# A two-mixer block with PEER experts: three edits of order and place, one of rate, one of sign

## The chip, the cores and the metric

The kernel runs on one core of a Trainium2 chip. The metric is the device time of one execution in microseconds (us). The engines are TensorE (PE, with its weight loads as PEld), VectorE (DVE), ScalarE (ACT) and GpSimd (POOL); SyncE (SP) and POOL issue the transfers. Each engine takes its own instructions strictly in the order in which they were laid down when the program was built.

## What the kernel computes

One layer over 512 tokens of width 1024, in float32. Sub-layer 1 is a norm, one wide projection, chunked band attention with a relative-position bias (8 heads of 64), an mLSTM (4 heads of 128), two gates and an output projection. Sub-layer 2 is a PEER layer: product keys choose 16 of 16,384 single-neuron experts per token and head.

```
s  = einsum("blhd,bkhd->bhlk", qj, kj) * scale + bias     # band attention
p  = softmax(where(valid, s, -inf))
...
q  = (xb @ w_pq).reshape(128, 8, 2, 128)                  # PEER, by blocks of 128 tokens
s_top, i_top = top_k(einsum("thpd,hpnd->thpn", q, sub_keys), 16)
best, ci     = top_k(s_top[:,:,0,:,None] + s_top[:,:,1,None,:], 16)
e    = i1 * 128 + i2                                      # i1, i2: the keys behind ci
gate = softmax(best)
act  = gelu(einsum("thkd,td->thk", u_exp[e], xb))
out  = rmsnorm(x + gt2 * einsum("thk,thkd->td", gate * act, v_exp[e]), final_g)
```

## The kernel before

Every float32 product on TensorE is made of three products of split operands: a tile is cast to a high part (`split`, line 147, ACT) and the rest is subtracted from it (line 150, DVE or POOL, tile `wlo`), and `mm3` (lines 160 to 162) multiplies high by high, high by low and low by high.

The first sub-layer takes the first 450 us or so. `mixer_a` does the attention, two heads per projection. For each head it loads a 128x512 bias, masks a corner of it with a memset (line 333), and for each of four row tiles adds bias and scores with a running maximum (line 343), negates the maximum (line 347), and exponentiates with it as the bias of the activation (line 349). The bias tile has two buffers.

The second sub-layer runs the experts in two ways. For tokens 160 to 511, 128 dense blocks, one per value of the first key, compute all 128 experts of the block (`hidden`: load `u_t[e]`, split, 24 matmuls into a 128x352 tile `ps_act`, gelu) and weigh them with a table of gates. For the other tokens rows of `u` and `v` are fetched one expert per token at a time, by an indirect transfer on POOL's queue (`row`, line 704) and a DVE instruction over 128x1024 elements for each (lines 712 and 761); the row buffers `ur` are five. The stages:

- `scores` finds the top experts, head by head. In `select` two masks of 128x1024 elements are multiplied on POOL (lines 691 and 699), with DVE instructions before and after each.
- `build` makes the gate table of 128 tokens: 32 steps for each of three token tiles (order 2, 3, 1). In each step DVE compares four tokens' first keys with an iota (line 781, tile `o4`), DVE, POOL and ACT make the second factor (lines 792 to 796, tile `oa`), TensorE multiplies (line 798, `ps_g`), ACT copies (line 799). Eight steps fill one buffer `gst`, which POOL's queue writes to memory `gd` (line 804).
- `ahead` does `hidden` for blocks 0 to 63 beside these two stages and stores the gelus in memory (`ad`). `paced` takes blocks at RATE_S = 1.1 per step of `scores` (17 steps, so 18 blocks), three more after it, and RATE_B = 0.4 per step of `build` (12 for each tile). 57 blocks are taken by then, and the last seven follow in a loop of their own (line 986), each with one step of the row gather `gathered(cp, 0)`.
- `output` goes over all 128 blocks, eight new ones (64 and up: "hot", `hidden` runs now, into one of two `ew` buffers of two blocks each) and eight stored ones ("cold") in turn. For each eight it loads a slice `gq` of the gate table from `gd` (line 844, SP's queue, two buffers), multiplies gelus and gates (line 859), splits them (lines 863 and 864), loads and splits `v_e[e]` (tile `vst`), and adds 18 matmuls of 128x512 to six accumulators. After each block it yields HOT = 2.6 or COLD = 1.25, the number of row steps that `paced` takes then.
- `finish` adds the residual to a token tile, norms and stores it. Tile 0 comes from the rows (259 steps: one for the index, 128 for `u`, one for the gelu, 128 for `v`, one for `finish`), tiles 1 to 3 from the accumulators, after the last block. Each call takes two 128x1024 buffers, `o` and `xr`, from the five of `ur`; two more hold `gt2` and the final gain from the first call on.

A list scheduler with a cost model lays down each engine's instructions: by order in the code where several are ready, otherwise whichever is ready, so that instructions may pass one another. `tc.issue_after(x)` keeps each instruction that it encloses, on the engine of x, behind x. `slowly(g)` runs a generator's steps under it with `state["mark"]`, which is the newest `wlo` of DVE.

Of the kernel before, what the change touches and what calls it, by code (L numbers as in the profile page):

```python
# [37 lines left out]
GG = 8  # L38
VST, UR = 3, 5
TG = 32  # L40
NR = P // TG
# [7 lines left out]
OAP, OAD, TWO = 8, 12, 4  # L49
RATE_S, TOP, RATE_G, RATE_B, RATE_0, RATE_A, HOT, COLD = 1.1, 3, 0.62, 0.4, 0.8, 1.0, 2.6, 1.25  # L50
WST, WB, VB = 4, 3, 3
# [23 lines left out]
def drive(*gens):  # L75
    for _ in weave(*gens):
        pass
# [3 lines left out]
def tile_block(  # L81
# [232 lines left out]
    def mixer_a(ap, hT, va, y_hi, y_lo):  # L314
# [7 lines left out]
        for hp in range(4):  # L322
            ps = bank("acc", "ps_qa")
            proj_t(ps, piece("qa", hp), hT)
            qaT = ap.tile([P, S], F32, tag="qaT", name="qaT", bufs=2)
            nc.scalar.mul(qaT, ps, 0.125)
            psy = bank("acc", "ps_ya")
            for hh in range(2):
                h = 2 * hp + hh
                po = 64 * hh  # L330
                bias = ap.tile([P, S], F32, tag="bias", name="bias", bufs=2)
                nc.sync.dma_start(bias, rel[h])
                nc.vector.memset(bias[:64, S - 64 :], NEG)
                for qt in range(4):
                    n = (qt + 1) * P
                    cs = slice(qt * P, n)
                    pss = bank("w", "ps_s")
                    nc.tensor.matmul(
                        pss[:, :n], qaT[po : po + 64, cs], kaT[po : po + 64, hp, :n], start=True, stop=True
                    )  # L340
                    sb = ap.tile([P, S], F32, tag="sb", name="sb", bufs=3)
                    mx = ap.tile([P, 1], F32, tag="mx", name="mx", bufs=3)
                    nc.vector.tensor_tensor_reduce(
                        out=sb[:, :n], in0=pss[:, :n], in1=bias[:, S - n :], scale=1.0, scalar=LOWEST,
                        op0=ALU.add, op1=ALU.max, accum_out=mx,
                    )
                    nc.vector.tensor_scalar_mul(mx, mx, -1.0)
                    sm = ap.tile([P, 1], F32, tag="sm", name="sm", bufs=3)
                    nc.scalar.activation(sb[:, :n], sb[:, :n], AF.Exp, bias=mx, accum_out=sm)
                    nc.vector.reciprocal(sm, sm)  # L350
                    nc.vector.tensor_scalar_mul(sb[:, :n], sb[:, :n], sm)
                    pst = bank("g", "ps_pt")
                    for kt in range(qt + 1):
                        nc.tensor.transpose(pst[:, kt * P : (kt + 1) * P], sb[:, kt * P : (kt + 1) * P], ident)
                    pt = ap.tile([P, S], F32, tag="pt", name="pt", bufs=2)
                    nc.scalar.copy(pt[:, :n], pst[:, :n])
                    for kt in range(qt + 1):
                        nc.tensor.matmul(
                            psy[po : po + 64, cs],
                            va[:, kt, h * 64 : (h + 1) * 64],  # L360
                            pt[:, kt * P : (kt + 1) * P],
                            start=kt == 0,
                            stop=kt == qt,
                        )
                    if qt % 2:
                        yield
            nc.scalar.copy(y_hi[:, 0, hp, :], psy)
            nc.vector.tensor_sub(y_lo[:, 0, hp, :], psy, y_hi[:, 0, hp, :].bitcast(F32))
            yield
# [283 lines left out]
    def select(cp, h, sv, i16, best, slots):  # L653
# [36 lines left out]
        nc.vector.tensor_tensor(out=m, in0=bc(pf), in1=bq(C_OFF), op=ALU.is_ge)  # L690
        nc.gpsimd.tensor_mul(q, m, bs(dl))
        both = cp.tile([P, 4, TOPK], F32, tag="both", name="both")
# [5 lines left out]
        nc.vector.tensor_tensor(out=m, in0=bc(of), in1=bq(C_SEQ), op=ALU.is_equal)  # L698
        nc.gpsimd.tensor_mul(m, m, bs(idx[:, :, 1, :]))
        nc.vector.tensor_reduce(slots[:, :, 1, h], m, axis=AX.X, op=ALU.add)  # L700
# [65 lines left out]
    def build(cp, i, slots):  # L766
# [8 lines left out]
        for b in range(P // TB):  # L775
            st = cp.tile([P, P, TB], F32, tag="gst", name="gst", bufs=2)
            for t4 in range(TB // 4):
                ps = bank("gw"[t4 % 2], "ps_g")
                o4 = cp.tile([P, 4, P], F32, tag="two", name="o4", bufs=TWO)
                t0 = b * TB + t4 * 4  # L780
                nc.vector.tensor_tensor(
                    out=o4, in0=iota.unsqueeze(1).broadcast_to([P, 4, P]),
# [31 lines left out]
    def ahead(up, h2T):  # L814

        for e in range(E1):
# [3 lines left out]
            if e % EG == EG - 1:  # L820
                nc.sync.dma_start(ad[e // EG], g)
            yield

    def output(cp, vp, h2T):
# [50 lines left out]
        for i in range(nt):  # L875
            with tc.issue_after(last.ins) if i else nullcontext():
                for n in range(2):
                    for x in late:
                        last = rows_of_v(i, n, *x)
            finish(cp, 1 + i, acc[2 * i : 2 * i + 2])  # L880

    def finish(cp, i, halves):

# [4 lines left out]
        gt2, fgb = state["rows"]  # L888
        o = cp.tile([P, D], F32, tag="ur", name="o", bufs=UR)
        xr = cp.tile([P, D], F32, tag="ur", name="xr", bufs=UR)  # L890
        nc.sync.dma_start(xr, x2d[i])
# [53 lines left out]
    def slowly(g):  # L945

        while True:
# [4 lines left out]
            yield  # L952

    def paced(main, *sides):

# [9 lines left out]
    with pool("epool") as cp:  # L965
# [3 lines left out]
        with pool("dpool") as dp, pool("upool") as up:  # L969
# [9 lines left out]
            for i in (2, 3, 1):  # L979
# [5 lines left out]
                drive((paced(build(dp, i, state["slots"][:, i]), (side, RATE_B), own), 1))  # L985
            drive((paced(side, (slowly(gather), RATE_A)), 1))
        if stop == "u":
# [76 lines left out]
```

## Time and profile before

| | |
|---|---|
| median of 3 runs | 1746.39 us |
| lowest, highest | 1742.57, 1746.93 us |
| profiled execution: its time | 1740.86 us |
| profiled execution: span, first to last instruction | 1739.1 us |
| PE busy in it | 1664.5 us (96%) |
| DVE, ACT, POOL busy | 1342.4, 769.4, 632.5 us |
| bytes moved | 441.00 MB |

Busy time of PE says that matmuls were under way, not that they ran at their best rate. The granted clock is the share of full speed (2.4 GHz) that TensorE was given; half of it is its other level, 1.2 GHz. The DMA share is the mean busy share of the core's 16 DMA engines. A number behind an arrow in square brackets is the time for which the engine stood idle just before, and what ended it.

### The profile page before, as it was taken

Reading aid. Unit: us, or ns where it says so; the run is one execution under the profiler, and the core shown is the slowest. Engines: PE = TensorE matmul, PEld = TensorE weight load, DVE = VectorE, ACT = ScalarE, POOL = GpSimd, SP = SyncE. Lnnn points to the kernel's source line nnn. Section 1 sums busy time; section 2 is a strip of 40 time slices with the busy share of each in tenths; the row PEclk is TensorE's granted clock in tenths of the full one; section 3 lists DMA queues with packets and bytes.
Section 4 is the critical chain, followed back from the end, with each engine's and each line's share of the span. In section 5 each row is a group of like instructions: output and inputs, shape, how many; then the busy total and the mean of one; then the engine's idle time right before and its main releaser. Section 6 shows DMA issues by size and latency. Waiting matters only on the chain.

```text
span 1739.1 us, 24668 instructions
## 1 busy us (share of the span) xinstructions
PE 1664.5 (96%) x8679; PEld 1446.8 (83%) x8679; DVE 1342.4 (77%) x2750; ACT 769.4 (44%) x1406; POOL 632.5 (36%) x524
## 2 busy tenths in 40 slices
PE   5999999999899998899999899999999999999996
PEld 4766678878789887899999788888888988888885
DVE  7467565675559999899798678787877878787896
ACT  4544545433453333889586233333333333333333
POOL 0000000000147765957483234444434434444450
PEclk9999999999999999999999899999999999999998
DMA  8524234572332333789979989999989999899984
GB/s 299 163 73 139 67 98 133 173 250 98 113 116 93 119 119 131 276 335 353 391 293 369 398 305 339 351 336 338 343 328 345 354 325 356 313 370 328 328 306 181
DMA packets 139166, 441.00 MB, mean 254 GB/s; under 512 B 15041, under 2 KB 41793, under 8 KB 137506
## 3 DMA queue, kind: packets, MB, share of 16 engines
q1 hardware_dynamic: 95842, 263.25, 43.4%
q0 software_dynamic: 43200, 176.18, 27.0%
q8 instruction: 68, 1.11, 0.3%
q14 instruction: 56, 0.46, 0.1%
HBM read 398.05 MB, written 40.90 MB: 252 GB/s over the span
## 4 chain that ended last, share of the span: by engine, by line
PE 55%; DVE 10%; DMA 3%; POOL 3%; issue 2%; ACT 0%; SPq 0%; DVEq 0%; POOLq 0%; ACTq 0%
PE acc L160 10%; PE acc L162 10%; PE acc L161 10%; PE ps_act L160 7%; PE ps_act L162 7%; PE ps_act L161 7%; PE ps_g L798 3%; DMA vst<-in_v_e 1%; DVE wlo L150 1%; POOL oa L796 1%; DMA ur<-in_u_r,eg 1%; DVE i L648 1%; DVE sc L649 1%; DVE i L651 1%; DMA gd<-gst 1%
## 5 line engine op out<-in xcount | busy, mean ns | idle before, releaser
L147 ACT CAST whi<-wst 128x512 fp32r<-128x512 f32 (+1 forms) x301 | 222.6, 771 | 402.2 <-PE ps_act L161 192.3
L162 PE MATMUL ps_act<-h2T_hi,wlo 128*128 128x352 f32 x1024 | 338.7, 331 | 14.6 <-DVE wlo L150 8.4
L160 PE MATMUL ps_act<-h2T_hi,whi 128*128 128x352 f32 x1024 | 337.0, 329 | 7.9 <-ACT ew L812 7.9
L161 PE MATMUL ps_act<-h2T_lo,whi 128*128 128x352 f32 x1024 | 337.0, 329 | 0.0
L150 DVE TENSOR_TENSOR wlo<-wst,whi 128x512 fp32r<-128x512 f32 (+1 forms) x251 | 235.0, 951 | 98.4 <-ACT whi L147 95.6
L161 PE MATMUL acc<-wlo,ehi 128*128 128x512 f32 x768 | 299.5, 390 | 0.0
L162 PE MATMUL acc<-whi,elo 128*128 128x512 f32 x768 | 290.4, 390 | 0.0
L704 POOL DMA_INDIRECT ur<-in_u_r,ei x128 | 181.0, 1414 | 252.5 <-DVE junk L712 222.1
L704 POOL DMA_INDIRECT ur<-in_v_r,ei x128 | 185.1, 1446 | 209.3 <-DVE sum_v L761 191.2
L160 PE MATMUL acc<-whi,ehi 128*128 128x512 f32 x768 | 252.7, 391 | 0.0
L162 PEld LDWEIGHTS ps_act<-h2T_hi,wlo 128*128 128x128 f32 x1024 | 195.5, 191 | 21.2 <-DVE wlo L150 10.7
L712 DVE SCALAR_TENSOR_TENSOR junk<-ur,h 128x1024 bf16<-128x1024 f32 x160 | 195.4, 1221 | 19.9 <-DMA ur<-in_u_r,eg 11.5
L160 PEld LDWEIGHTS ps_act<-h2T_hi,whi 128*128 128x128 f32 x1024 | 195.7, 191 | 12.2 <-ACT ew L812 8.5
L161 PEld LDWEIGHTS ps_act<-h2T_lo,whi 128*128 128x128 f32 x1024 | 195.6, 191 | 3.8
L150 DVE TENSOR_TENSOR wlo<-vst,whi 128x1024 fp32r<-128x1024 f32 x128 | 155.7, 1222 | 25.8 <-ACT whi L147 25.6
L147 ACT CAST whi<-vst 128x1024 fp32r<-128x1024 f32 x128 | 132.2, 1047 | 94.7 <-PE acc L162 39.9
L161 PEld LDWEIGHTS acc<-wlo,ehi 128*128 128x128 f32 x768 | 144.2, 188 | 28.6
L162 PEld LDWEIGHTS acc<-whi,elo 128*128 128x128 f32 x768 | 144.0, 188 | 28.7
L160 PEld LDWEIGHTS acc<-whi,ehi 128*128 128x128 f32 x768 | 142.9, 188 | 26.6
L761 DVE SCALAR_TENSOR_TENSOR sum_v<-ur,act,sum_v 128x1024 f32<-128x1024 f32 x127 | 163.0, 1283 | 1.7 <-DMA ur<-in_v_r,ei 0.6
L863 ACT CAST ehi<-gq 128x768 fp32r<-128x768 f32 x64 | 53.4, 837 | 233.4 <-PE acc L161 199.9
L150 POOL TENSOR_TENSOR wlo<-wst,whi 128x512 fp32r<-128x512 f32 x50 | 67.3, 1361 | 163.3 <-ACT whi L147 163.3
(302 smaller groups left out, 2856.7 us busy)
## 6 DMA issues: line engine op xcount, KB each, us to landing
wst<-in_u_t SPq DMA_DIRECT2D x128, 512.0 KB, 5.5
vst<-in_v_e SPq DMA_DIRECT2D x128, 512.0 KB, 6.7
wst<-in_w_pieces SPq DMA_DIRECT2D x76, 512.0 KB, 3.7
wst<-in_w_ada SPq DMA_DIRECT2D x48, 512.0 KB, 3.4
gd<-gst POOLq DMA_DIRECT2D x12, 2048.0 KB, 10.6
gq<-gd SPq DMA_DIRECT2D x16, 1536.0 KB, 12.3
ad<-gelu SPq DMA_DIRECT2D x16, 704.0 KB, 6.6
aq<-ad SPq DMA_DIRECT2D x16, 704.0 KB, 7.3
```

The costliest lines, as they stand in the source:

```text
L147: nc.scalar.copy(hi[:, cs], t[:, cs])
L150: ins = e.tensor_tensor(out=lo[:, cs], in0=t[:, cs], in1=hi[:, cs].bitcast(F32), op=ALU.subtract)
L160: nc.tensor.matmul(o, a[0], b[0], start=first, stop=False)
L161: nc.tensor.matmul(o, a[0], b[1], start=False, stop=False)
L162: return nc.tensor.matmul(o, a[1], b[0], start=False, stop=last)
L648: nc.vector.max_index(places[:, :8], vals[:, :8], data)
L649: nc.vector.match_replace(data, vals[:, :8], data, LOWEST)
L704: nc.gpsimd.indirect_dma_start(out=t, out_offset=None, in_=src, in_offset=bass.IndirectOffsetOnAxis(ap=ei[:, j : j + 1], axis=0))
L712: nc.vector.scalar_tensor_tensor(junk(), row(cp, u_r, ei, j), 1.0, h2, op0=ALU.mult, op1=ALU.mult, accum_out=act[:, j : j + 1])
L761: nc.vector.scalar_tensor_tensor(sum_v, t, act[:, j : j + 1], sum_v, op0=ALU.mult, op1=ALU.add)
L798: nc.tensor.matmul(ps[:, tt::4], oa, ob, start=True, stop=True)
L863: nc.scalar.copy(whb, w)
```

## The change

It has five parts.

1. The last three blocks of `ahead` (`BACK`) are taken in a loop of their own without row steps. In it every DVE instruction stands behind the last compare of the last table (line 781, now kept as `state["built"]`). Four blocks, not seven, are left for the loop with row steps.
2. HOT goes from 2.6 to 2.85 and COLD from 1.25 to 1.4.
3. In `finish` for token tiles 2 and 3 the two buffers `o` and `xr` are the halves of a buffer `gq` instead of two of the `ur`.
4. In `select` the two multiplications of the last head go to DVE.
5. The attention works with negated scores: the query is scaled by -0.125, the bias is negated by POOL after its load, the maximum becomes a minimum, the exponential gets scale -1, and the negation of the maximum is dropped. The corner's memset goes to POOL.

```diff
+TG, BACK = 32, 3
-... HOT, COLD = ... 2.6, 1.25
+... HOT, COLD = ... 2.85, 1.4
 # mixer_a
-            nc.scalar.mul(qaT, ps, 0.125)
+            nc.scalar.mul(qaT, ps, -0.125)
...
-                nc.vector.memset(bias[:64, S - 64 :], NEG)
+                nc.gpsimd.tensor_scalar_mul(bias, bias, -1.0)
+                nc.gpsimd.memset(bias[:64, S - 64 :], -NEG)
...
-                        out=sb[:, :n], in0=pss[:, :n], in1=bias[:, S - n :], scale=1.0, scalar=LOWEST,
-                        op0=ALU.add, op1=ALU.max, accum_out=mx,
+                        out=sb[:, :n], in0=pss[:, :n], in1=bias[:, S - n :], scale=1.0, scalar=-LOWEST,
+                        op0=ALU.add, op1=ALU.min, accum_out=mx,
                     )
-                    nc.vector.tensor_scalar_mul(mx, mx, -1.0)
-                    nc.scalar.activation(sb[:, :n], sb[:, :n], AF.Exp, bias=mx, accum_out=sm)
+                    nc.scalar.activation(sb[:, :n], sb[:, :n], AF.Exp, scale=-1.0, bias=mx, accum_out=sm)
 # select
-        nc.gpsimd.tensor_mul(q, m, bs(dl))
+        e = nc.vector if h == 7 else nc.gpsimd
+        e.tensor_mul(q, m, bs(dl))
...
-        nc.gpsimd.tensor_mul(m, m, bs(idx[:, :, 1, :]))
+        e.tensor_mul(m, m, bs(idx[:, :, 1, :]))
 # build
-                nc.vector.tensor_tensor(
+                state["built"] = nc.vector.tensor_tensor(
 # ahead
+            state["ahead"] = e + 1
             yield
 # output
-            finish(cp, 1 + i, acc[2 * i : 2 * i + 2])
+            room = None
+            if i:
+                gq = vp.tile([P, nb, GG, TB], F32, tag="gq", name="gq")
+                room = [gq[:, 4 * j : 4 * j + 4].rearrange("p b i t -> p (b i t)") for j in range(2)]
+            finish(cp, 1 + i, acc[2 * i : 2 * i + 2], room)
 # finish(cp, i, halves, room=None)
-        o = cp.tile([P, D], F32, tag="ur", name="o", bufs=UR)
-        xr = cp.tile([P, D], F32, tag="ur", name="xr", bufs=UR)
+        o, xr = room or [cp.tile([P, D], F32, tag="ur", name=nm, bufs=UR) for nm in ("o", "xr")]
+    def until(g, e):
+        while state["ahead"] < e:
+            yield next(g)
 # the main sequence
-            drive((paced(side, (slowly(gather), RATE_A)), 1))
+            drive((paced(until(side, E1 - BACK), (slowly(gather), RATE_A)), 1))
+            state["mark"] = state["built"].ins
+            drive((slowly(side), 1))
```

## Rows read from the trace of the kernel before

**Rows 1.** The page's first line: span and instructions.

```profile
span 1739.1 us, 24668 instructions
```

**Rows 2.** Stretches: us, busy of PE, PEld, DVE, ACT, POOL; clock; DMA share; GB/s.

```profile
100.00:250.00 150.00, 144.56 (x661) 99.37 (x661) 95.27 (x298) 70.39 (x182) 1.27 (x2) 0.97 0.29 92
...
941.00:985.00 44.00, 34.43 (x188) 33.09 (x188) 27.56 (x35) 14.61 (x20) 15.03 (x12) 0.88 1.03 385
985.00:1719.00 734.00, 734.00 (x3634) 642.89 (x3633) 588.65 (x631) 255.17 (x306) 314.76 (x219) 1.00 0.92 333
1650.00:1700.00 50.00, 50.00 (x251) 43.88 (x250) 46.46 (x41) 16.25 (x20) 27.60 (x20) 1.00 0.86 303
1719.00:1739.10 20.10, 6.52 (x29) 5.07 (x27) 12.41 (x24) 5.23 (x15) 0.00 (x0) 0.76 0.36 127
...
970.00:980.00 10.00, 4.24 (x14) 4.24 (x15) 5.92 (x7) 5.49 (x8) 0.63 (x1) 0.58 1.06 379
...
800.00:850.00 50.00, 50.00 (x361) 49.78 (x362) 49.06 (x97) 41.82 (x97) 25.88 (x23) 1.00 1.01 401
```

**Rows 3.** Instructions in order of time on PE, 945 to 985: those after idle time.

```profile
951.18 0.43 PE L160 MATMUL ps_act<-h2T_hi,whi 128*128 128x352 f32 x1 [1.34 <-ACT ew L812]
...
965.43 0.43 PE L162 MATMUL ps_act<-h2T_hi,wlo 128*128 128x352 f32 x1 [1.66 <-DVE wlo L150]
...
975.76 0.66 PE L160 MATMUL ps_act<-h2T_hi,whi 128*128 128x352 f32 x1 [6.57 <-ACT ew L812]
```

**Rows 4.** Instructions in order of time on DVE, 915 to 1000.

```profile
926.15 1.22 DVE L150 TENSOR_TENSOR wlo<-wst,whi 128x1024 fp32r<-128x1024 f32 x1
...
932.93 0.68 DVE L781 TENSOR_TENSOR o<-iota,sT 128x512 f32<-128x512 f32 x1
...
933.79 1.21 DVE L150 TENSOR_TENSOR wlo<-wst,whi 128x1024 fp32r<-128x1024 f32 x1
...
963.01 1.23 DVE L712 SCALAR_TENSOR_TENSOR junk<-ur,h 128x1024 bf16<-128x1024 f32 x1 [0.64 <-DMA ur<-in_u_r,ei]
...
973.59 1.69 DVE L859 TENSOR_TENSOR gq<-ew,gq 128x704 f32<-128x704 f32 x2 [5.94 <-DMA gq<-gd]
```

**Rows 5.** Instructions in order of time on POOL, 900 to 1000.

```profile
941.26 0.57 POOL L804 DMA_DIRECT2D gd<-gst  x1 [0.76 <-ACT gst L799]
...
957.51 0.93 POOL L704 DMA_INDIRECT ur<-in_u_r,ei  x1 [6.93 <-DVE junk L712]
...
964.51 1.68 POOL L704 DMA_INDIRECT ur<-in_u_r,ei  x1 [0.94 <-DVE junk L712]
```

**Rows 6.** Issues in order of time on SP's queue, 880 to 1000.

```profile
953.40 0.39 SPq L844 DMA_DIRECT2D gq<-gd  x1
```

**Rows 7.** The page's part 6: issues, KB each, median us to landing.

```profile
gq<-gd SPq DMA_DIRECT2D x16, 1536.0 KB, 12.3
```

**Rows 8.** Instructions in order of time on DVE, 1685 to 1740.

```profile
1719.66 1.29 DVE L895 TENSOR_TENSOR o<-acc,gt 128x512 f32<-128x512 f32 x2 [3.10 <-PE acc L162]
...
1730.05 1.29 DVE L895 TENSOR_TENSOR o<-acc,gt 128x512 f32<-128x512 f32 x2 [1.66 <-DMA out<-o]
...
1734.26 1.41 DVE L904 SCALAR_TENSOR_TENSOR o<-o,rs,fgb 128x512 f32<-128x512 f32 x2
```

**Rows 9.** Instructions in order of time on ACT, 1690 to 1740.

```profile
1712.19 1.28 ACT L900 ACT_TABLE_LOAD   x1
```

**Rows 10.** Instructions in order of time on POOL, 668 to 703.

```profile
689.10 3.25 POOL L699 TENSOR_TENSOR m<-m,idx 128x1024 f32<-128x1024 f32 x1 [6.83 <-DVE m L698]
```

**Rows 11.** Instructions in order of time on DVE, 668 to 703.

```profile
692.38 1.22 DVE L700 TENSOR_REDUCE slots<-m 128x64 f32<-128x1024 f32 x1 [2.29 <-POOL m L699]
```

**Rows 12.** Groups of DVE, 60 to 250: busy us, mean ns, idle before.

```profile
L347 DVE TENSOR_SCALAR mx<-mx 128x1 f32<-128x1 f32 x32 | 4.6, 148 | 0.3
```

**Rows 13.** Groups of POOL by shape, whole span.

```profile
L150 POOL TENSOR_TENSOR wlo<-wst,whi 128x512 fp32r<-128x512 f32 x50 | 67.3, 1361 | 163.3 <-ACT whi L147 163.3
...
L468 POOL TENSOR_SCALAR_AFFINE_SELECT mbd<-mbc 128x512 f32<-128x512 f32 x4 | 2.8, 700 | 321.6 <-ACT mbc L466 321.6
```

More of the change, by code (lines that the diff above doesn't have):

```diff
@@ L39 @@
 VST, UR = 3, 5
-TG = 32
+TG, BACK = 32, 3
 NR = P // TG
@@ L49 @@
 OAP, OAD, TWO = 8, 12, 4
-RATE_S, TOP, RATE_G, RATE_B, RATE_0, RATE_A, HOT, COLD = 1.1, 3, 0.62, 0.4, 0.8, 1.0, 2.6, 1.25
+RATE_S, TOP, RATE_G, RATE_B, RATE_0, RATE_A, HOT, COLD = 1.1, 3, 0.62, 0.4, 0.8, 1.0, 2.85, 1.4
 WST, WB, VB = 4, 3, 3
@@ L879, in output, with finish @@
                         last = rows_of_v(i, n, *x)
-            finish(cp, 1 + i, acc[2 * i : 2 * i + 2])
-    def finish(cp, i, halves):
+            room = None
[3 more added lines that the diff above has]
+            finish(cp, 1 + i, acc[2 * i : 2 * i + 2], room)
+    def finish(cp, i, halves, room=None):
         if "rows" not in state:
```

## The prediction

> **What bounds the kernel now.** I read the busy times by stage first, then what PE waited for, then each engine's order around the two places where PE stands still. From 985 to 1719 us PE is busy for all of 734 us, with DVE at 589 and a DMA share of 0.92 [rows 2]: there the matmuls set the time, and an edit to another engine gains nothing as long as PE stays fed. The time that PE loses lies elsewhere. Between 941 and 985, the handover from the tables to the output, it works 34.4 of 44 us [rows 2]. Its three waits there are 1.34, 1.66 and 6.57 us, 9.57 in sum [rows 3]. After the long one the granted clock averages 0.58 over ten us, below full speed and towards 1.2 GHz [rows 2], and the first matmul takes 0.66 us, its like before 0.43 [rows 3]. From 1719 on PE works 6.5 of 20.1 us, because only the last three token tiles' `finish` is left [rows 2]. Between 100 and 250, the attention, it loses 150 - 144.56 = 5.4 us [rows 2]. These three places are what the change can win.
>
> The sum is made against the profiled execution, 1740.86 us: its span of 1739.1 [rows 1] and 1.8 around it. The median of the runs is 5.5 us above it, so the sum's difference is set against 1746.39.
>
> **Part 1, the held blocks.** PE's long wait ends when `gq` lands: DVE multiplies at 973.59 after 5.94 us of waiting for it [rows 4], which frees the `ew` buffer that PE's queue waits for [rows 3]. `gq` is issued at 953.40 [rows 6], as soon as the last piece of the table, issued at 941.26 [rows 5], is in memory. It lands 973.59 - 953.40 = 20.2 us later against a median of 12.3 [rows 7]. So two things can bring it forward: an earlier table, and fewer transfers beside it.
>
> The table. The last compare stands at 932.93, the `wlo` of the last three blocks at 926.15, 933.79 and one more after that [rows 4]: two of the three stand behind the compare already, and the edge moves one block. It takes 1.22 us out of DVE's way to the compare [rows 4], or, where PE's order sets the table's end, the block's 24 matmuls: 188 took 34.43 us there [rows 2], 0.18 each, so 4.4 us at most. I take 3, nearer to PE's figure, because the table's last copy releases the write only at 941.26, 8 us after the compare.
>
> The transfers. Seven row steps go with the last seven blocks now, four after. Each fetches 128x1024 elements of 4 bytes, 0.52 MB; three fewer are 1.57 MB, and at the 385 GB/s of this stretch, whose DMA share is 1.03 [rows 2], that is 4.1 us. These are just the fetches that stand beside `gq`: four are issued from 957.51 to 964.51 [rows 5]. The row instruction at 963.01 that waited for one of them [rows 4] also held the `wlo` behind PE's 1.66 us.
>
> Together `gq` lands 7 us earlier. The total of PE work ready before it is unchanged, so the idle 9.6 us shrink by about 7. The slow clock is worth some 2 us more (14 matmuls in 4.24 us, 0.30 each, against 0.18, for the 14 [rows 2]); I leave it out because part of the 7 may be lost to the same full DMA. Bounds: 0, where `gq` comes no sooner, and 11.6, where waits and slow clock vanish. SP's queue takes `gq` in its place among the loads of `u`; held blocks keep three of four load buffers a little longer, which is hidden as long as PE has these three blocks (3 x 4.4 = 13 us) to do.
>
> **Part 3, the tail.** Tile 1's first instruction starts at 1719.66, and DVE then goes on to 1730.05, where tile 3 starts after 1.66 us of waiting for a store of an earlier tile, because its `o` needs a freed row buffer [rows 8]. Its last instruction starts at 1734.26 and takes 1.41 [rows 8], so its chain is 1735.67 - 1730.05 = 5.6 us. In the `gq` buffers the wait goes: 1.66. If the scheduler also puts tile 3's first four instructions (2 x 1.29) before tile 2's last pair (1.41 with its own short wait), the chain overlaps with it, up to 2 us more. So 1.7 to 3.6; I take 2.5. What is late next is DVE: three tiles of about 4.3 us from 1719.66 on.
>
> One thing goes against it. Tile 0's `finish` comes earlier (part 2), before the last gelus. ACT then loads the square root's table twice, for tile 0 and again for tile 1. Now it is loaded at 1712.19, for 1.28 us [rows 9], under the matmuls. In the tail it would stand between tile 1's squares and its root, where DVE has tile 2 to do: 0, at most 1.3. It lies in the choice of 2.5 over 3.6.
>
> **Part 2, more rows per block.** Before, 32 of 259 steps are taken ahead of the output, 227 are left, and 16 blocks take 8 x 2.6 + 8 x 1.25 = 30.8: they end at block 117 of 128. After, 230 are left at 34 per 16 blocks, and end at block 107. DVE gains 3.2 x 1.23 = 3.9 us of work [rows 4] per 16 blocks, which take 734/8 = 92 us: from 80% to 84%. From 1650 to 1700 it is at 93% with PE at 50 of 50 [rows 2], so it has that room. The DMA gains 3.2 x 0.52 = 1.7 MB per 92 us, 18 GB/s: from 333 to 351, against 401 with PE fully busy at 800 to 850 [rows 2]. Cost taken: 0. The other end: if full share carried only 333/0.92 = 362 GB/s, 351 still fits on average, but the cold blocks, with 18 matmuls against a hot block's 42 and 1.4 rows each, would not. I price that at the extra bytes' own time, 1.7 MB / 0.362 = 4.6 us per 16 blocks over 107 blocks, at most 31 us if nothing were hidden. A third of it, 10 us, is what I would expect if the DMA did bound, since hot blocks leave room again.
>
> **Part 4, the last head on DVE.** POOL's second multiplication takes 3.25 us [rows 10], and DVE waits 2.29 of it [rows 11]. On DVE two such instructions cost about 2 x 1.22, by the subtraction over as many elements [rows 4]. That is 2.4 more work against 2.3 less waiting: 0, between -2.3 (both hidden by other work) and +2.4 (the wait came from elsewhere).
>
> **Part 5, the sign.** DVE loses 32 negations of 0.148 us, 4.6 in all [rows 12], and eight small memsets. POOL gains eight instructions over 128x512; its nearest rows take 0.70 (one input) and 1.36 us (two) [rows 13]. POOL works 1.3 of these 150 us [rows 2], and the bias is loaded one head ahead into the other buffer, which hides them; were a head to wait for each, it would be 8 x 1.4 = 11. PE loses 5.4 us in this stretch [rows 2] and DVE is at 64%, so only a part of DVE's gain reaches PE: 1 of 4.6; bounds -4.6 and +11.
>
> The multiplication by POOL on the last head took 3.25 us [rows 10] while DVE worked beside it on instructions with two inputs. By the Trainium skill, page "SBUF — State Buffer", section "Who interferes with whom", a VectorE instruction with two SBUF inputs and a GpSimd instruction that reads SBUF block each other for the whole instruction. By that, up to eight times 1.4 us of DVE's attention work would be held, a third of it on the path (+4), and part 5 would come to about +3 and the sum to -6.5; DVE's idle third leads me to take the row's side.
>
> **Sum.** -7 (handover), -2.5 (tail), 0 (rows), 0 (last head), -1 (sign): -10.5. The profiled execution would take 1730.4, and the median 1746.4 - 10.5, so 1736. As the scheduler lays out every engine anew, some 4 us either way are added to the bounds.
>
> **Rivals.**
> *The handover does not move.* Two blocks are behind the compare already, and the DMA is full (1.03 [rows 2]), so what leaves `gq`'s way is replaced by loads of `u` and `v`. Against it: the four fetches beside it are real [rows 5] and only rows are paced. Tail and sign alone: -3.5, 1743.
>
> *The handover closes.* `gq` lands before PE runs dry; the waits and the slow clock go: -11.6 - 2.5 - 1 = -15, 1731. The 20.2 us against 12.3 speak for it; a share of 1.03 all through speaks against.
>
> *The DMA bounds the output* (slower). From the handover on the transfers are full; each fetch put in per block delays a load that PE needs, and the 10 us of part 2 come on top, with nothing gained at the handover: +10 - 2.5 = +7.5, 1754. It decides from the point where the cold blocks' demand stays above what the engines carry for longer than three `v` buffers last. For it: share 0.92 already. Against it: 401 GB/s beside a busy PE, and PE without a wait in 734 us [rows 2]. [...]
>
> *Not what it says.* If the held blocks were done before the compare by the order alone, part 1 would change only the three fetches: -4 - 2.5 - 1, 1739, inside the forecast's range.
>
> **Chances.** Forecast 0.55, with its own range 1731 to 1741; closes 0.12; does not move 0.20; DMA bounds 0.13. A measurement here can tell 0.3%, 5.2 us, from no change, so faster means below 1741.2. The first two lie there, and a sixth of the third: 0.70. Same is the rest of the third, 0.17; slower 0.13. The range 1728 to 1748 leaves out the slower rival and little else.
>
> **What would show it.** PE's waits between 930 and 985 fall from 9.6 to about 3 and the first matmuls after them take 0.43; `gq` lands within 16 us of its issue and the table's last write is issued some 3 us before its old place; tile 3's `finish` starts without a wait for a store; the last fetch of rows lies some 60 us before the end; PE still has no wait in the output. Waits of PE for `wlo` or `whi` there, behind loads of `vst`, would prove the slower rival; an unchanged wait of 6 us for `ew` the first.

## The result, and the profile after

The changed kernel took 1723.68 us in the median of five runs (1722.48 to 1730.54), the kernel before beside it 1745.93 (1742.57 to 1746.93): a ratio of 0.9882 with the 95% interval 0.9863 to 0.9902. In a second measurement, the run `all` below, it took 1725.33 against 1743.32: 0.9895 [0.9874, 0.9917]. So the change gains 18 to 22 us. 10.5 were predicted, and 1723.68 lies below the range, which began at 1728.

The runs of one kernel differ by up to 13 us, the slower ones mostly at a lower mean granted clock (`only_h7` below has three at 1724.7 to 1726.4 with a clock of 0.988 and three at 1734.5 to 1737.5 with 0.982 to 0.985), so a difference of 2 us between medians is not read here. The first profile of the changed kernel (1730.54, span 1728.8) had a granted clock of 0.90 between 100 and 250 us, where the kernel before had 0.97. The division by stages is therefore read from the run `all`, the same kernel, span 1723.3, beside the kernel before. Each row is a stage: up to the first matmul of `scores`; to the first transpose of `build`; to the issue of the last piece of the table; to the first multiplication by `gq`; to the first `finish` from the accumulators; to the end. The columns are those of [rows 2].

Before:

```profile
0.00:471.60 471.60, 441.53 (x1992) 339.76 (x1992) 293.19 (x700) 209.91 (x453) 9.61 (x18) 0.98 0.45 148
471.60:687.20 215.60, 201.57 (x1084) 180.72 (x1082) 191.47 (x902) 84.88 (x164) 128.86 (x157) 0.98 0.34 111
687.20:941.30 254.10, 246.75 (x1761) 245.59 (x1762) 229.42 (x460) 199.63 (x449) 164.33 (x120) 0.99 0.87 327
941.30:973.60 32.30, 24.89 (x150) 24.02 (x149) 16.36 (x23) 8.09 (x11) 11.63 (x10) 0.97 1.02 386
973.60:1719.70 746.10, 743.94 (x3672) 652.24 (x3673) 599.60 (x644) 261.69 (x315) 318.11 (x220) 0.99 0.92 334
1719.70:1739.10 19.40, 5.82 (x26) 4.50 (x24) 12.37 (x24) 5.23 (x15) 0.00 (x0) 0.75 0.35 131
```

The changed kernel, run `all`:

```profile
0.00:472.90 472.90, 442.57 (x1992) 340.15 (x1993) 293.16 (x662) 210.09 (x453) 24.23 (x34) 0.98 0.43 148
472.90:687.10 214.20, 201.05 (x1092) 180.54 (x1092) 191.70 (x900) 88.11 (x168) 123.81 (x156) 0.98 0.35 114
687.10:934.70 247.60, 243.19 (x1725) 242.78 (x1726) 230.00 (x463) 197.40 (x447) 162.39 (x120) 0.98 0.88 332
934.70:964.20 29.50, 28.16 (x169) 27.87 (x168) 13.25 (x17) 9.49 (x13) 7.68 (x6) 1.00 1.02 392
964.20:1707.20 743.00, 742.64 (x3683) 650.83 (x3682) 602.78 (x650) 262.11 (x315) 333.42 (x223) 1.00 0.92 338
1707.20:1723.30 16.10, 5.86 (x26) 4.50 (x24) 12.15 (x24) 5.01 (x15) 0.00 (x0) 0.83 0.26 98
```

The span is 15.8 us shorter, and the differences of the stages add up to it: +1.3, -1.4, -6.5, -2.8, -3.1, -3.3. The largest is that of the tables (third row), but it is in good part work that has gone to other stages: PE has 36 matmuls fewer to do there (1725 for 1761) and 19 more in the handover. The time for which PE stands still, stage less busy time, does not change when a block moves. By it the differences are +0.3, -0.9, -2.9, -6.1, -1.8 and -3.3, and PE is busy for 1.0 us less in all. So the handover with the output behind it gives 7.9 us, the tail 3.3, and the tables 2.9 (7.4 to 4.4), a stage for which the prediction has no term but the 3 us of the held block.

The rows of the first profile after that answer to [rows 2], the handover and the output:

```profile
940.00:984.00 44.00, 42.41 (x240) 40.35 (x240) 27.81 (x35) 15.56 (x21) 11.22 (x9) 1.00 1.03 393
985.00:1712.60 727.60, 727.60 (x3608) 637.72 (x3607) 587.53 (x632) 255.21 (x307) 330.84 (x220) 1.00 0.92 337
```

PE's only wait from 930 to 990 in the first profile after, in order of time, where [rows 3] had three:

```profile
955.33 0.43 PE L160 MATMUL ps_act<-h2T_hi,whi 128*128 128x352 f32 x1 [1.34 <-ACT ew L813]
```

The issue of `gq` on SP's queue and the multiplication that waits for it, as in [rows 6] and [rows 4]:

```profile
956.75 0.39 SPq L846 DMA_DIRECT2D gq<-gd  x1
```

```profile
969.65 1.69 DVE L861 TENSOR_TENSOR gq<-ew,gq 128x704 f32<-128x704 f32 x2 [3.90 <-DMA gq<-gd]
```

And POOL's issues there, as in [rows 5]:

```profile
940.19 0.57 POOL L805 DMA_DIRECT2D gd<-gst  x1 [0.88 <-ACT gst L800]
...
952.22 0.94 POOL L705 DMA_INDIRECT ur<-in_u_r,ei  x1 [0.30 <-issue]
975.90 1.42 POOL L705 DMA_INDIRECT ur<-in_u_r,ei  x1 [22.74 <-DVE junk L713]
```

`gq` is there 969.65 - 956.75 = 12.9 us after its issue (20.2 before), no row fetch is issued in that time (four were before), the waits of 1.66 and 6.57 us are gone, and the clock stays at 1.00. What moved between the issue of `gq` and its landing, before (953.4 to 973.6) and in `all` (951.2 to 964.2); q0 is POOL's queue, which has only row fetches then:

```profile
DMA packets 3333, 8.04 MB, mean 398 GB/s; under 512 B 219, under 2 KB 1755, under 8 KB 3333
q0 software_dynamic: 1197, 4.33, 54.6%
```

```profile
DMA packets 2526, 5.08 MB, mean 390 GB/s; under 512 B 135, under 2 KB 1671, under 8 KB 2526
q0 software_dynamic: 381, 1.36, 26.1%
```

The rate is nearly the same, and the other queue moved 3.7 MB both times. The rows' 2.97 MB less are 7.5 us at 398 GB/s, and `gq` came 7.2 us sooner. Fetches issued before `gq` still move beside it.

### The profile page after: what moved, and what is told of

It reads as the page before. It is cut to its first block, busy times and chain, and to the rows that moved or that the text cites. A ratio compares the mean times of both kernels' runs of the same rounds, so it can differ in the third digit from the quotient of the medians.

```text
span 1728.8 us, 24663 instructions
## 1 busy us (share of the span) xinstructions
PE 1669.0 (97%) x8679; PEld 1449.4 (84%) x8679; DVE 1343.9 (78%) x2712; ACT 772.0 (45%) x1408; POOL 651.6 (38%) x538
## 4 chain that ended last, share of the span: by engine, by line
PE 58%; DVE 8%; DMA 3%; POOL 2%; issue 1%; ACT 1%; SPq 0%; DVEq 0%; POOLq 0%; ACTq 0%
PE acc L160 10%; PE acc L161 10%; PE acc L162 10%; PE ps_act L162 7%; PE ps_act L160 7%; PE ps_act L161 7%; PE ps_g L799 4%; DVE wlo L150 1%; DMA vst<-in_v_e 1%; DVE sc L649 1%; DMA gd<-gst 1%; DVE i L651 1%; DVE i L648 1%; DVE v L647 1%; DVE v L650 1%
## 5 line engine op out<-in xcount | busy, mean ns | idle before, releaser
L150 DVE TENSOR_TENSOR wlo<-wst,whi 128x512 fp32r<-128x512 f32 (+1 forms) x251 | 239.5, 968 | 100.8 <-ACT whi L147 98.9
L705 POOL DMA_INDIRECT ur<-in_u_r,ei x128 | 193.4, 1511 | 240.7 <-DVE junk L713 200.0
L713 DVE SCALAR_TENSOR_TENSOR junk<-ur,h 128x1024 bf16<-128x1024 f32 x160 | 195.3, 1221 | 15.8 <-DMA ur<-in_u_r,eg 11.1
```

The lines of the kernel that those rows point to most:

```text
L150: ins = e.tensor_tensor(out=lo[:, cs], in0=t[:, cs], in1=hi[:, cs].bitcast(F32), op=ALU.subtract)
L705: nc.gpsimd.indirect_dma_start(out=t, out_offset=None, in_=src, in_offset=bass.IndirectOffsetOnAxis(ap=ei[:, j : j + 1], axis=0))
L713: nc.vector.scalar_tensor_tensor(junk(), row(cp, u_r, ei, j), 1.0, h2, op0=ALU.mult, op1=ALU.mult, accum_out=act[:, j : j + 1])
```

## The experiments

Every kernel was timed in five rounds or more against the kernel before, whose median was 1743.3 to 1743.7 in all of these. The table has the median, the ratio to the kernel before, two stretches of the profiled run, `scores` (second stage above) and tables to output (stages three to five), and the time for which PE stands still in the latter. Part 2 was not taken away from the full change.

| run | what it is | median us | ratio [95%] | scores | tables to output | PE idle there |
|---|---|---|---|---|---|---|
| before | | 1743.5 | 1 | 215.6 | 1032.5 | 16.9 |
| all | the change | 1725.33 | 0.9895 [0.9874, 0.9917] | 214.2 | 1020.1 | 6.1 |
| no_hold | without part 1 | 1735.15 | 0.9947 [0.9925, 0.9970] | 212.9 | 1032.6 | 15.8 |
| hold_rows | queued, but rows beside all seven blocks | 1731.33 | 0.9929 [0.9915, 0.9942] | 214.7 | 1027.8 | 13.4 |
| few_rows | rows beside four blocks, not queued | 1725.57 | 0.9895 [0.9880, 0.9911] | 214.4 | 1019.4 | 6.9 |
| no_room | without part 3 | 1726.45 | 0.9900 [0.9878, 0.9922] | 214.6 | 1019.0 | 7.6 |
| no_h7 | without part 4 | 1726.16 | 0.9894 [0.9878, 0.9911] | 214.4 | 1021.4 | 7.3 |
| no_sign | without part 5 | 1727.04 | 0.9905 [0.9883, 0.9926] | 215.0 | 1014.6 | 4.4 |
| only_hold | before and part 1 | 1739.89 | 0.9975 [0.9963, 0.9986] | 215.5 | 1030.0 | 14.8 |
| only_rate | before and part 2 | 1743.34 | 0.9994 [0.9980, 1.0008] | 216.9 | 1037.2 | 18.9 |
| only_room | before and part 3 | 1740.67 | 0.9983 [0.9972, 0.9995] | 217.1 | 1033.8 | 16.2 |
| only_h7 | before and part 4 | 1730.45 | 0.9931 [0.9905, 0.9957] | 215.2 | 1019.5 | 7.9 |
| only_sign | before and part 5 | 1731.23 | 0.9922 [0.9901, 0.9943] | 215.3 | 1023.4 | 10.7 |
| h3 | part 4 on head 3 instead | 1744.68 | 1.0006 [0.9994, 1.0018] | 218.3 | 1033.3 | 17.4 |
| h7m | half of part 4 | 1740.93 | 0.9980 [0.9967, 0.9992] | 217.2 | 1031.0 | 14.8 |
| top2 | before, order alone changed | 1737.59 | 0.9962 [0.9947, 0.9977] | 216.7 | 1028.3 | 13.4 |
| oap3 | before, order alone changed | 1734.47 | 0.9947 [0.9933, 0.9961] | 217.4 | 1024.2 | 11.0 |
| all_top2 | the change in the old start of the tables | 1730.56 | 0.9931 [0.9911, 0.9951] | 213.9 | 1026.0 | 13.7 |
| no_work | the order and parts 1 to 3, without 4 and 5 | 1730.41 | 0.9926 [0.9911, 0.9941] | 216.9 | 1020.3 | 8.1 |

**The change again, and without one part each.** `no_hold` has the old loop, `no_room` an `if False:` ahead of the `gq` buffer, `no_sign` and `no_h7` the lines of before.

> The changed kernel once more, for a second profile and times beside the three below. Theory A (handover and tail): PE's idle time at the handover near 1.6 us again and in the tail near 10.4; the slow clock between 110 and 150 us of the first profile (mean 0.76, 0.92, 0.50, 0.90 in four stretches of 10 us) is chance and is gone, span 1720 to 1722, and 1.2% below the kernel before. Theory B (the sign): the slow clock in the attention comes with the new sign, and stands there again. Theory C (layout): the gain outside handover and tail is the scheduler's new order, the same in each profile of this kernel.

> The change without part 1: the last seven blocks of ahead with a row step each, as before. Theory A: PE's idle time at the handover comes back to 8 to 10 us with the slow clock after it, 8 to 12 us slower than the full change (about 1733). Theory C: another order moves other stages by several us either way, so the difference is not the handover's. Rival of the hold: the rates or the other parts moved gq, and leaving the hold out costs under 3 us.

> The change without part 3: all finish buffers from ur. Theory A: tile 3 waits for a store again, 3 us slower than the full change (about 1727), nothing else moves. Rival: the later rows end just before the tail in both, so buffers of ur are the same and the tail is the same within 1 us.

> The change without part 5: attention with the old sign. Theory A: within 3 us of the full change, PE idle 100 to 250 near 5.4 us. Theory B: the sign's shorter chain on DVE carries the missing 10 us, so this is 8 to 10 us slower (about 1733). Theory C: as A for the attention, but the order of scores and tables changes and moves them by several us.

> The change without part 4: the last head's two multiplications on POOL again. Theory A (prediction): within 2 us of the full change. Theory D (the last head carries the 6 us by which the tables ended sooner in every variant so far): the last write of the table is issued 254 us after the first slot transposes, as before, not 247, and the kernel is 5 to 7 us slower than the full change (1731).

Only the removal of part 1 costs much, some 10 us. Parts 3, 4 and 5 can each be taken away for 1 to 2 us, within the spread of the runs; for part 3 the profile is sharper: from the first `finish` to the end `no_room` takes 19.4 us, as before, the full change 16.1.

**One part each on the kernel before.**

> The kernel before with part 1 alone. The order of all engines is the old one up to the last table, so this is the hold on the old layout. Theory A: PE idle at the handover 1.5 to 3 us instead of 9.6, no slow clock after it, 8 to 11 us faster than before (1733). Theory C (layout): the old layout had only one of the 64 blocks left behind the table's last write, so the hold moves two blocks here and wins as much or more. If fewer fetches alone count, gq lands 13 us after its issue.

> The kernel before with part 3 alone; the order differs only in the last 40 instructions of DVE. Theory A: tile 3 starts without the wait for a store, tail 16 us instead of 19.4 from tile 1's first instruction to the end, 3 us faster than before (1740.5).

> The kernel before with part 2 alone. PE, ACT and POOL get the same order as before, DVE's differs only among rows and their neighbours in the output, so whatever the theory, the same as before within 1 us, with the last row instruction at the same distance from the end (36 us) as before; the prediction had put that distance at 60.

> The kernel before with part 5 alone. Theory A (prediction): -1 us, between -4.6 and +11. Theory C: its own work is worth under 2 us in the attention (PE idle 5 to 6 us there, as in every profile so far), but the order of scores and tables is laid out anew, and the tables take 240 to 248 us instead of 254, with two or three blocks left behind their last write: 5 to 10 us faster than before (1736).

> The kernel before with part 4 alone. Theory A: the same as before within 2 us. Theory D: the tables take 247 us instead of 254, 5 to 7 us faster than before. If the layout is what moves the tables, this may differ from D in either direction.

Alone they gain 4, 3, 0, 12 and 13 us: 32 in sum where the change gains 18. The two that were costed at 1 and 0 gain most, and the full change does almost as well without either. (The 13 of `only_h7` is the median of runs from 1724.7 to 1737.5.) So in part they win the same thing. Where? The attention, where the sign's work is, has PE idle for 4.82 us of 100 to 250 in `only_sign` (5.44 before), and the table shows the gain elsewhere: between the tables and the end of the output, in which no instruction of part 5 lies, it saves 9.1 us, `only_h7` 13.0; 6.2 and 9.0 of that are time for which PE no longer stands still.

**What the held blocks do.** Part 1 both queues the last three blocks and takes away their row steps.

```diff
 # hold_rows: queued, with rows
-            drive((slowly(side), 1))
+            drive((paced(slowly(side), (slowly(gather), RATE_A)), 1))
 # few_rows: without rows, not queued
-            state["mark"] = state["built"].ins
-            drive((slowly(side), 1))
+            drive((side, 1))
```

> The change with the queueing behind the last compare kept, but each of the last three blocks has its row step again. Theory A1: like the change without part 1 (1735), gq lands 18 us or more after its issue, PE idle about 8 us at the handover. Theory A2: only 4 us of the 10 are lost, 1729.

> The change with the row steps of the last three blocks dropped as in it, but without the queueing behind the last compare. Theory A1 (only the three fewer fetches matter, since the scheduler puts the last blocks behind the compare anyway): like the full change within 2 us (1725), gq lands 13 us after its issue, PE idle at the handover under 2.5 us. Theory A2 (the queueing matters, the prediction's 3 of 7 us): 3 to 5 us slower than the full change.

Without the queueing nothing is lost (1725.57 for 1725.33); with it but with the rows, 6 us of the 10 are. So the queueing keeps 4 us where rows stay (`no_hold` 1735.15, `hold_rows` 1731.33), between the two theories, and brings nothing once they are gone. In `hold_rows` the fetches stand beside `gq` again (issued at 945.99), in order of time on POOL:

```profile
947.54 0.94 POOL L705 DMA_INDIRECT ur<-in_u_r,ei  x1 [5.15 <-DVE junk L713]
950.12 0.94 POOL L705 DMA_INDIRECT ur<-in_u_r,ei  x1 [1.64 <-DMA ur<-in_u_r,ei]
952.68 1.68 POOL L705 DMA_INDIRECT ur<-in_u_r,ei  x1 [1.62 <-DVE junk L713]
```

and PE, in order of time, waits until the product of `gq` frees a buffer `ew`:

```profile
965.63 0.66 PE L160 MATMUL ps_act<-h2T_hi,whi 128*128 128x352 f32 x1 [5.60 <-ACT ew L813]
```

**The order at the start of the tables.** What the two parts have in common stands in the order laid down. In the kernel before, and in `only_rate`, `only_room` and `only_hold`, POOL has eight `oa` ahead of its first row fetch, and PE's last table matmul stands with half a block left to do behind it (1.4 with part 1). In `only_sign` and `only_h7` it is two and three `oa`, and two blocks or more; in the full change none, and 1.8. The start, in order of time on all engines, before:

```profile
694.72 14.05 POOL L796 TENSOR_SCALAR oa<-iota,sT 128x128 f32<-128x128 f32 x8 [2.37 <-ACT sT L772]
...
708.95 1.18 POOL L704 DMA_INDIRECT ur<-in_u_r,eg  x1 [0.18 <-issue]
...
713.46 1.23 DVE L712 SCALAR_TENSOR_TENSOR junk<-ur,h 128x1024 bf16<-128x1024 f32 x1 [7.26 <-DMA ur<-in_u_r,eg]
...
715.45 1.13 PE L798 MATMUL ps_g<-o,oa 128*128 128x128 f32 x4 [5.10 <-DVE o L781]
```

The fetch waits for 14 us of POOL's work, DVE for the fetch, and PE, which needs DVE's next compare, stands still for 5.10 us. The 14 us are not POOL's work alone. In the columns of [rows 2], the first five `oa` and the last three:

```profile
694.72:706.43 11.71, 11.71 (x86) 11.71 (x85) 11.48 (x26) 11.42 (x29) 11.71 (x5) 1.00 0.77 243
706.50:708.70 2.20, 2.20 (x19) 2.20 (x18) 0.00 (x0) 2.20 (x5) 2.20 (x3) 1.00 0.00 0
```

With DVE at work beside them five took 11.71 us, the longest of them 4.85; with DVE idle the last three took 0.79 each. Transfers do not explain it: in `top2` an `oa` took 0.81 us beside an idle DVE with a DMA share of 1.05.

In the full change no `oa` stands ahead of the fetch, and PE waits for the `oa` themselves, here in `all`:

```profile
708.51 1.16 PE L799 MATMUL ps_g<-o,oa 128*128 128x128 f32 x8 [1.97 <-POOL oa L797]
712.11 1.65 PE L799 MATMUL ps_g<-o,oa 128*128 128x128 f32 x6 [2.44 <-POOL oa L797]
```

So of the 5.10 us only 0.7 are won at this place there, and 1.6 in the first profile after. A wait of 4.4 to 5.1 us for a compare, between 715 and 721, stands in the kernel before, `only_hold`, `only_room`, `only_rate`, `h3` and `h7m`, all with eight `oa` ahead, and in no other.

The next four kernels part this order from the work. `top2` takes two blocks instead of three between `scores` and `build`, which changes the order and no arithmetic; `h3` moves the work of part 4 at another head, which leaves the start and the end of the tables as before; `h7m` has the old start and 2.2 blocks at the end; `all_top2` is the whole change in the old start.

```diff
 # top2, all_top2
-... RATE_S, TOP, ... = 1.1, 3, ...
+... RATE_S, TOP, ... = 1.1, 2, ...
 # h3 (both multiplications), on the kernel before
+        e = nc.vector if h == 3 else nc.gpsimd
 # h7m, on the kernel before
-        nc.gpsimd.tensor_mul(m, m, bs(idx[:, :, 1, :]))
+        (nc.vector if h == 7 else nc.gpsimd).tensor_mul(m, m, bs(idx[:, :, 1, :]))
```

> The kernel before with one number changed: two blocks instead of three are taken between scores and build (TOP 3 to 2). No instruction is added, removed or moved to another engine, but in the order laid down POOL has two oa instead of eight ahead of its first row fetch, and two blocks instead of half a block stand behind the tables' last matmul, as in the changed kernel. Theory 'layout': it gains what the sign and the last head each gained alone, some 12 us: 1731 (1727 to 1736), PE idle between 700 and 925 at most 4 us instead of 7.1, first transpose to last table write 240 to 247 us instead of 254. Rival 'own work' (the removed negations and the quicker last head made the gain): 1743.5, as before, within 3 us.

> The kernel before with the two multiplications of head 3 instead of the last head on DVE: the same amount of work moved, but in the order laid down POOL still has eight oa ahead of its first row fetch and half a block is left behind the last table, as before. Theory 'layout': no gain, 1743.5 (1740 to 1746). Rival 'own work': such a move gains what the last head's gained, 1731.

> The kernel before with only the last head's second multiplication on DVE. In the order laid down the start of the tables is the old one (eight oa ahead of the first fetch), and 2.2 blocks are left behind the last table's matmuls, as in the changed kernel. It parts the two halves of the layout. If the start of the tables makes the gain: 1740 to 1743, with PE's wait of 5 us near 715 kept. If the blocks left at the end make it: 1731 to 1735, with PE idle at the handover 4 to 6 us. Both by half: 1737.

> The whole change with TOP 2: everything the change does is kept, but in the order laid down POOL has eight oa ahead of its first row fetch again, and 1.3 blocks behind the last table, so the old start of the tables. Theory 'layout': it loses what the layout gives beside the other parts, about 18 - 9 = 9 us: 1734 (1731 to 1738), with PE's wait of some 5 us near 715 back. Rival 'own work': 1725, as the whole change.

The order without work gains 6 us, half of what was expected of it; the work without the order gains nothing (`h3`); the end without the start gains 3; and the change in the old start loses 5 of its 18. But `all_top2` does not lose it at the start: its eight `oa` take 9.5 us, DVE waits 3.0 us for the fetch instead of 7.26, and no wait of PE between 684 and 925 is over 1.5 us: the expected wait of 5 us is not there. It loses at the handover, where PE stands still for 8.1 us instead of 1.7, with 17.5 us for `gq` and 3.02 MB of rows beside it. So eight `oa` ahead of the fetch are not enough for the wait, and this run does not price the start. Its long wait, on PE:

```profile
966.32 2.93 PE L160 MATMUL acc<-whi,ehi 128*128 128x512 f32 x6 [6.80 <-ACT ehi L865]
```

The start of `top2` in the same view:

```profile
698.28 5.92 POOL L796 TENSOR_SCALAR oa<-iota,sT 128x128 f32<-128x128 f32 x2 [2.37 <-ACT sT L772]
704.39 1.18 POOL L704 DMA_INDIRECT ur<-in_u_r,eg  x1 [0.18 <-issue]
...
708.83 1.23 DVE L712 SCALAR_TENSOR_TENSOR junk<-ur,h 128x1024 bf16<-128x1024 f32 x1 [4.87 <-DMA ur<-in_u_r,eg]
...
711.56 0.57 PE L798 MATMUL ps_g<-o,oa 128*128 128x128 f32 x2 [1.94 <-DVE oa L796]
```

DVE's first row comes 4.6 us earlier, though the tables began 2.6 us later, and PE's wait falls from 5.10 to 1.94.

**Order or work for the other half.** `oap3` gives POOL three `oa` buffers instead of eight (`OAP, OAD, TWO = 3, 12, 4` on the kernel before). `no_work` is the changed kernel with TOP 2 and without parts 4 and 5.

> The changed kernel without the sign and without the last head on DVE, but with TOP 2 instead of 3: no arithmetic differs from the kernel before, only places and rates, and in the order laid down POOL has two oa ahead of its first row fetch, with 1.9 blocks behind the last table, as good as in the changed kernel (none, 1.8). Theory 'layout': 1725 (1722 to 1729), as the whole change. Rival 'own work counts too': the sign's and the last head's shares are missing, 4 to 6 us: 1730 (1728 to 1734).

> The kernel before with one number changed: three instead of eight buffers for POOL's oa (OAP 8 to 3), so POOL can't lay more than three ahead. No arithmetic and no engine changes. In the order laid down three oa stand ahead of the first row fetch and 2.2 blocks behind the last table. If that order is worth what it was worth with TOP 2: 1736 to 1738. If it is worth what sign and last head gained alone: 1731. If fewer buffers stall PE for oa in the tables: 1743 or more.

`oap3` gains 9 us by the order alone, and PE stands still for 5.9 us less from the tables to the output, nearly what `only_sign` gains there (6.2). `no_work` reaches 1730.4, the rival's figure, 5 short of the change. Its stages from the tables on are the change's (1020.3 for 1020.1); its `scores`:

```profile
474.10:691.00 216.90, 204.22 (x1092) 183.50 (x1092) 191.18 (x904) 85.50 (x165) 127.68 (x155) 0.97 0.34 112
```

What it lacks in these profiles lies ahead of them: `scores` takes 216.9, 2.7 more. PE does not stand still longer there (12.7 us for 13.2); it is busy 3.2 us longer for the same 1092 matmuls, at a clock of 0.97 for 0.98. Over all kernels `scores` takes 212.9 to 215.3 us with part 4 or 5 whole, and 215.5 to 218.3 in the nine others, groups only 0.2 us apart with one profile for nearly all of them. Whether the work of the two parts makes the 5 us is not shown. Nor is which feature of the order makes 4 us in `top2` and 13 in `only_h7` between the tables and the end of the output; the profiled runs took 1738.94 and 1726.44, on either side of their medians, and by the time for which PE stands still the two are 3.5 and 9.0. No version tried beats the changed kernel clearly; `few_rows` equals it without the queueing.

## Why the prediction was wrong

In the terms of the sum, by the time for which PE stands still in the two profiles: handover -7.9 for -7, tail -3.3 for -2.5, first sub-layer with the sign +0.3 for -1, and `scores` and tables -3.8, for which the sum has nothing. With PE busy for 1.0 us less this is the 15.8 of the profiles; the medians differ by 18 to 22.

**The handover (-7 forecast).** PE's idle time from 925 to 990 fell from 9.57 to 1.7: the rival *the handover closes* nearly came true here, at 1.00 of clock, and the 2 us of slow clock that the sum left out belonged in it. That the forecast's 3 + 4 came so near is luck. The fetches were the right cause and too small: three were priced at the time of their bytes, 4.1 us, but 2.97 MB less of rows moved beside `gq`, nearly six fetches, and it landed 7.3 us sooner, 12.9 for 20.2, nearly the median of [rows 7]. The other step was wrong: queueing behind the compare brings nothing beside that (`few_rows`). An earlier table does not bring `gq` forward as far either. In `all` the last write is issued at 934.67, 6.6 us sooner, but `gq` at 951.23, only 2.2: before, SP's queue waited 0.7 us for the table, and in `all` not at all; there `gq` stands behind three loads of `u`, which wait for `wlo`. SP's waits between 942 and 962, the one for the table before and the one for `wlo` in `all`:

```profile
SPq L844 <- DMA gd<-gst: 0.7, 1, 0.7
```

```profile
SPq L135 <- DVE wlo L150: 8.4, 3, 3.5
```

As *not what it says* had it, only the fetches count, but they count for the whole handover, and in the full change part 1 is worth 10 us; alone on the kernel before it is worth 4, and `gq` is still 17.4 us on its way there, with 2.48 MB of rows beside it. In 15 of these profiles the first `gq` took 12.7 to 20.2 us, for 4.96 to 8.04 MB at 390 to 398 GB/s.

**The tail (-2.5).** 3.3, within 1.7 to 3.6. Tile 3's first instruction (1717.68) no longer waits for a store; it stands before tile 2's last pair (1721.91). The second table load on ACT that was weighed against this is not there: the one load stands at 1705.16, under the matmuls. DVE in order of time in the first profile after, where both tiles are named `gq` after their buffers:

```profile
1712.63 1.29 DVE L900 TENSOR_TENSOR o<-acc,gt 128x512 f32<-128x512 f32 x2 [3.10 <-PE acc L162]
...
1717.68 0.68 DVE L900 TENSOR_TENSOR gq<-acc,gt 128x512 f32<-128x512 f32 x1
...
1721.91 1.41 DVE L909 SCALAR_TENSOR_TENSOR gq<-gq,rs,fgb 128x512 f32<-128x512 f32 x2
...
1723.95 1.41 DVE L909 SCALAR_TENSOR_TENSOR gq<-gq,rs,fgb 128x512 f32<-128x512 f32 x2
```

**The rows (0).** The cost is right, `only_rate` 0.9994, and the slower rival with it refuted: no wait of PE in the output, DMA share 0.92. The reason was wrong. The gather should have ended 60 us before the end; its last row is summed at 1697.10 of 1728.8, 16 us ahead of the first `finish`, as before. In `only_rate` the orders of PE, ACT and POOL are those of the kernel before to the last instruction: the rate of the generator did not move them.

**The last head (0) and the sign (-1): the step that failed.** As work both were small, as forecast. The multiplication and the sum behind it, where [rows 11] showed a wait of 2.29 us, in `only_h7` on DVE:

```profile
688.00 1.22 DVE L700 TENSOR_TENSOR m<-m,idx 128x1024 f32<-128x1024 f32 x1
690.28 1.21 DVE L701 TENSOR_REDUCE slots<-m 128x64 f32<-128x1024 f32 x1
```

And the attention loses no less PE time with the sign turned (5.83 us of 100 to 250 in `all`, 5.44 before). The bias took POOL 1.67 us, not 1.4, and was hidden. The prediction weighed up to eight times 1.4 us of DVE's attention work held by it, and set that aside; the eight full-width additions of bias and scores could not show it, since none of them stands beside a negation in `all`. By the rule of the Trainium skill, page "SBUF — State Buffer", section "Who interferes with whom", a VectorE instruction with two SBUF inputs and a GpSimd instruction that reads SBUF hold each other up. The trace agrees, at other instructions and for little time: of two equal passes over 128x1024 elements on DVE the one inside a negation took 1.63 us, the other 1.22, and the negations took 1.57 to 1.97 us beside DVE and 1.49 with DVE idle. The same shows in the 14 us of the eight `oa` above, in the wait that the sum left out. POOL's negations in `all`, 60 to 250 us, two of them in order of time, and the two passes on DVE:

```profile
L333 POOL TENSOR_SCALAR bias<-bias 128x512 f32<-128x512 f32 x6 | 10.0, 1671 | 147.4 <-DMA bias<-in_rel 147.4
```

```profile
176.21 1.49 POOL L333 TENSOR_SCALAR bias<-bias 128x512 f32<-128x512 f32 x1 [17.12 <-DMA bias<-in_rel]
194.32 1.77 POOL L333 TENSOR_SCALAR bias<-bias 128x512 f32<-128x512 f32 x1 [16.42 <-DMA bias<-in_rel]
```

```profile
170.34 1.22 DVE L175 SCALAR_TENSOR_TENSOR junk<-wst,srow 128x1024 bf16<-128x1024 f32 x1
194.66 1.63 DVE L175 SCALAR_TENSOR_TENSOR junk<-wst,srow 128x1024 bf16<-128x1024 f32 x1
```

What failed is the sentence on the scheduler, "some 4 us either way", which put the order at nothing in the sum. Each of the two edits alone makes it lay down the tables and the blocks anew, and this goes with 9 to 13 us from the tables on; order changes without any work are worth 6 and 9 in the median, and the same work at another head, with the old order, nothing (`h3`). So the order is shown to make gains of this size; that it makes all of the 12 and 13 is not shown. In the full change it is worth less: PE stands still for 3.8 us less in `scores` and tables. The 5.10 us wait at 715 was in the trace before, in a stage that the prediction passed over because no edit lies in it. Eight `oa` that DVE slows, ahead of a fetch that DVE waits for, are an accident of the order, and so the first thing that any edit ahead of it can move.

## What to carry to other kernels

Where a scheduler lays down the order, an edit's own work is only one term: list the waits that come from the order itself, wherever they stand, and hold a part of their sum as a possible gain of any edit ahead of them: here PE stood still for 7.4 us in the tables, and the kernels with another start lost 2 to 5 of them. Time one edit without work beside the real ones (here TOP 2, 6 us) before crediting an edit with its gain. Where the DMA engines are busy throughout, price a transfer that everything waits for by all the bytes that move between its issue and its landing, those of fetches issued earlier among them: here 8.04 MB in 20.2 us and 5.08 in 13.0.

## What the runs showed beside that

On POOL an `oa` of 128x128 took from 0.81 to 4.91 us in `top2`, the same instruction six times apart:

```profile
L796 POOL TENSOR_SCALAR oa<-iota,sT x48: 805/1389/4908, 698.3 to 897.3; 128x128 f32<-128x128 f32 x48
```

The three figures are least, median and most, in ns; the longest is the first of the pair at 698.28, the shortest one that stood beside an idle DVE. And the gains of single parts, 32 us in sum, overstate the change's 18, while the losses on removal, 10 + 1 + 1 + 2, understate it: neither list alone says what a part is worth.
